# Both heads of a pair in one 128x128 chain matmul, two buffers each for R and K, and new durations in the planner

## The chip, the cores and the metric

The kernel runs on one core of a Trainium2 chip. Five engines of that core work at the same time, each on its own queue: TensorE (PE, matrix multiplications), VectorE (DVE), ScalarE (ACT), GpSimd (POOL) and SyncE (SP), which here issues nearly all the DMA transfers. The time is device microseconds (us) of one execution, and a kernel's time is the median over several executions.

## The reference

One layer of a hybrid encoder trunk takes a step for 512 prompt tokens of a new stream and for 8 running streams of 16 tokens each, 640 tokens in all, model width 1024. All is float32.

```python
h    = rmsnorm(x, norm_g)
proj = h @ w_in                      # columns: q,k,v,z_A | gates g_A,g_B | r,k,v,w-lora,a-lora,z_B
# A: stick-breaking attention, 16 heads of 64
z = q @ k.T / 8
weight[t,s] = sigmoid(z[t,s]) * prod(1 - sigmoid(z[t,j]) for s < j < t)      # s < t only
o_a = weight @ v                     # sample streams also see 128 cached keys
# B: RWKV-7, 16 heads of 64, after a token shift of its columns; w, kk, a from small projections
for t: S = S * w_t - (S kk_t)(kk_t * a_t) + v_t k_t ;  o_t = S r_t
o_b = groupnorm(o_b) + bonus
y   = x + (sig(g_A) * ((o_a silu(z_A)) @ w_o_a) + sig(g_B) * ((o_b silu(z_B)) @ w_o_b)) @ w_out
# out: rmsnorm(y), keys and values, shift rows, the states S
```

## The kernel before

**The projections.** The large products are cut into 97 jobs of 128 output columns. A job loads its weights (`raw`, 128x1024), splits them into a rounded part `whi` (ScalarE) and the rest `wlo` (VectorE, `wlow`), and runs over two halves of the tokens; each half is 8 k-steps of three matmuls, `xh` by `whi`, `xl` by `whi` and `xh` by `wlo`, 128x320, into a PSUM bank `ps_g`. In the trace these are the rows `ps_g<-xh,whi`, `ps_g<-xl,whi` and `ps_g<-xh,wlo`, called projection matmuls below. The weights of the job after this one are split while this one runs: `wlow` is emitted at k-step 5 of the first half.

**The recurrence.** RWKV-7 is computed in chunks of 64 tokens, for a pair `p` of heads at a time (eight pairs; head 0 on partitions 0 to 63, head 1 on 64 to 127). For each pair four generators, here called streams, run:

- `prep`: from the projected `R`, `K`, `V` and the decays to `H` (the decayed keys and queries), `BK` (both kinds of keys, written beside each other), then the intra-chunk products `BK` x `H` on PE, which VectorE masks into `AB` and into the other half of `H`; last the transposes `X` and `BKt`. Between the products stand the norm (`nrm`, `bones`) and the latent matmuls (`wh`, `wl`).
- `prep2`: the inverse of a triangular matrix per chunk. ScalarE copies diagonal blocks of `AB` into `STG`, VectorE turns them (`INV`), GpSimd solves them in small steps, VectorE turns them back into `STG`, PE combines the blocks ("the solve").
- `samp`: the states of the sample streams.
- `chain`: the serial part, one `step` per chunk (the first step takes chunks 0, 8 and 9 together, so 8 steps and 10 chunks). Each step visits PE three times: `X` by `H` into `ps_b` and `ps_c`; after ScalarE has copied the result to `RH`, `RH` by `AB` into `ps_b`; after ScalarE has copied that into `X`, `X` by `BKt` into `ps_b` and `X` by `AB` into `ps_c`. VectorE then forms the next chunk's state in `X` (with `SW`, the decayed old state), and the next step starts. Each product is done per head, as two 64-column matmuls; `ps_c` gathers the outputs, which ScalarE moves to `Oa` after four steps.

`post` then normalises `Oa`. When all pairs are done, the attention follows in the same manner (`aprep`, `attn`): scores `ks` by `qh` and `ql` into `ps_a`, sigmoids `kp` and `bt` on ScalarE, a running product and `bt` times `kp` on VectorE, transposes of `bt` into `ps_b` (a multiplication by the identity in `cst`), and the product with the values. Then come the output projections.

**What sets the order.** The queues hold a fixed program. It is written by a planner: `Clock` (lines 89 to 155) keeps a modelled time for each engine and tile, `_Eng.call` (from line 211) charges a duration for each emitted instruction, and `Driver.run` (from line 283) takes, at PE's modelled time, the stream of the lowest number whose tiles are ready by the model; if none is, it emits the next two k-steps of a projection job. The durations in `Clock` thus place instructions in the queues, and do nothing else. `near` in it is the delay that it takes between two instructions that depend on each other on one engine; `take` gives the next PSUM bank (3 of `ps_g`, 2 each of `ps_a` and `ps_b`, 1 of `ps_c`). A stream can also wait for a flag: `prep` begins when the pair before has set `rkfree`, since `R` and `K` have one buffer each, and the projection jobs of the next pair's `R`, `K` and `V` come up once `rksoon` is set:

```python
        if p > 2:
            yield flag("chain", p - 3)                     # before H is written (three buffers)
...
            g1, s1k = ([], []) if p == 0 else ([("rkfree", p - 1)], [("rksoon", p - 1)])
...
                    if (half, k) == ((0, 5) if i else (1, 1)):
                        wlow(i + 1)
```

Of the kernel before, what the change touches and what calls it, by code (L numbers as in the profile page):

```python
# [33 lines left out]
T = 640  # L34
# [54 lines left out]
class Clock:  # L89
# [114 lines left out]
class _Eng:  # L204
# [3 lines left out]
    def __getattr__(self, op):  # L208
        f = getattr(self.obj, op)

        def call(*a, **k):
# [7 lines left out]
            if e == "pe":  # L219
                w = k.get("lhsT")  # L220
                if w is None:
                    d = 0.115
                else:
                    m = _cols(w)
                    if w.dtype == F32R:
                        d = max(n / 2360.0, 0.107)
                    elif w.dtype == F32:
                        d = max(0.026 + n * 0.00087, 0.082 if m > 32 else 0.041) if m <= 64 else 0.005 + n / 600.0
                    else:
                        d = 0.06  # L230
            elif e == "act":
                d = 0.05 + n * 0.00086 + 0.1 * sum(hasattr(k.get(x), "tensor") for x in ("scale", "bias"))
# [6 lines left out]
            elif e == "dve":  # L239
                d = 0.066 + n * 0.00105  # L240
                if "scalar" in op:
                    d += 0.03 * sum(hasattr(x, "tensor") and _cols(x) == 1 for x in list(a) + list(k.values()))
                if op == "reciprocal":
                    d = 0.05 + n * 0.0064
            elif e == "pool":
                d = 0.15 + n * (0.0021 if op == "tensor_tensor" else 0.001)
                if op == "tensor_copy":
                    d = 0.2 + n * 0.0035
# [72 lines left out]
def body(tc, ins, outs, dbg=None):  # L321
# [157 lines left out]
    def gemm_range(i0, i1):  # L479
# [6 lines left out]
        for i in range(i0, i1):  # L486
# [9 lines left out]
            for half in range(2):  # L496
# [5 lines left out]
                for k in range(8):  # L502
# [12 lines left out]
                    if (half, k) == ((0, 5) if i else (1, 1)):  # L515
                        wlow(i + 1)
# [29 lines left out]
    def start():  # L546
        x34 = pers.tile([128, 2, D], F32, tag="H", name="x34", bufs=3)
        srow = pers.tile([88, 3, 128], F32, tag="AB", name="srow", bufs=3)
# [159 lines left out]
    def prep(p):  # L708
# [9 lines left out]
        if p + 1 < NPAIR:  # L718
            rw[p + 1] = {}
# [16 lines left out]
        yield [K]  # L736
        nrm = tr.tile([128, T], F32, tag="nrm", name="nrm")
# [28 lines left out]
        setf("rksoon", p)  # L766
# [10 lines left out]
        if p > 2:  # L777
            yield flag("chain", p - 3)
            yield flag("schain", p - 3)
        H = o["H"] = pers.tile([128, 2, 10, 128], F32, tag="H", name="H", bufs=3)  # L780
        AB = o["AB"] = pers.tile([128, 10, 128], F32, tag="AB", name="AB", bufs=3)
        BK = tr.tile([128, 10, 2, 64], F32, tag="BK", name="BK")
        c8 = dict(c=8)
        for h in range(2):
            rs = RS[h]
            stt(H[rs, h, 0:8, 0:64], kkn[rs, 0:512].rearrange("p (c t) -> p c t", **c8), -1.0,
                e1p[rs, :, 0:64], ALU.mult, ALU.mult)
            stt(H[rs, h, 8:10, 0:64].rearrange("p g (b t) -> p g b t", b=4),
                kkn[rs, 512:640].rearrange("p (g b t) -> p g b t", g=2, b=4), -1.0,
                e1s[rs, :, 0:16].rearrange("p (g b) t -> p g b t", g=2), ALU.mult, ALU.mult)  # L790
# [15 lines left out]
        for c0, c1 in ((0, 4), (4, 8), (8, 10)):  # L806
# [3 lines left out]
            for c in range(c0, c1):  # L810
                for h in range(2):
                    rs = RS[h]
                    mm(pvs[h][:, c - c0, :], lhsT=BK[rs, c].rearrange("p s t -> p (s t)"),
                       rhs=H[rs, h, c, :], start=True, stop=True)
            for h in range(2):
                rs, op = RS[h], RS[1 - h]
                vtt(AB[rs, c0:c1, :], pvs[h][rs, 0:n],
                    msk[rs].unsqueeze(1).broadcast_to([64, n, 128]), ALU.mult)
                vtt(H[op, h, c0:c1, :], pvs[h][op, 0:n],
                    msk[op].unsqueeze(1).broadcast_to([64, n, 128]), ALU.mult)  # L820
            yield [H]
# [37 lines left out]
    def prep2(p):  # L859
# [17 lines left out]
        tmp = inv.tile([128, 128], F32, tag="itmp", name="itmp")  # L877
# [11 lines left out]
        for q in range(4):  # L889
# [11 lines left out]
        for c in range(8):  # L901
            for q in range(4):
                up = slice(32 * q, 32 * q + 16)
                i = 32 * (q % 2)
                mm(pv[32 * q:32 * q + 32, c], lhsT=AB[up, c, i:i + 32], rhs=Q[up, 0:16, c],
                   start=True, stop=True)
        Y1 = inv.tile([128, 8, 16], F32, tag="itmp", name="Y1")
# [24 lines left out]
        yield [AB, Q]  # L932
# [4 lines left out]
        for c in range(8):  # L937
            for h in range(2):
                a = slice(64 * h, 64 * h + 32)
                b = slice(64 * h + 32, 64 * h + 64)  # L940
                mm(psy[b, c * 32:(c + 1) * 32], lhsT=AB[a, c, 32:64], rhs=Q[a, :, c],
# [7 lines left out]
        for c in range(8):  # L949
            for h in range(2):  # L950
                a = slice(64 * h, 64 * h + 32)
                b = slice(64 * h + 32, 64 * h + 64)
                mm(pst[a, c * 32:(c + 1) * 32], lhsT=Y[b, c, :], rhs=AB[b, c, 32:64],
                   start=True, stop=True)
        for h in range(2):
            a = slice(64 * h, 64 * h + 32)
            V.tensor_copy(AB[a, 0:8, 32:64], pst[a, 0:256].rearrange("p (c s) -> p c s", c=8))
        setf("prep", p)

    def samp(p):  # L960
# [17 lines left out]
        for b in range(8):  # L978
            for h in range(2):
                rs = RS[h]  # L980
                hv = H[rs, h, 8 + b // 4, :].rearrange("p (e b t) -> p e b t", e=2, b=4)
                mm(pv[rs, b], lhsT=S0T[rs, b, :], rhs=hv[:, :, b % 4, :], start=True, stop=True)
        for h in range(2):
            rs = RS[h]
            for g in range(2):
                act(out=H[rs, h, 8 + g, :].rearrange("p (e b t) -> p e b t", e=2, b=4),
# [6 lines left out]
    def chain(p):  # L993
# [11 lines left out]

        def step(js, pos):

# [3 lines left out]
            rh = ps[:, 0:192].rearrange("p (c v) -> p c v", c=3)  # L1011
            u = ps[:, 192:384].rearrange("p (c v) -> p c v", c=3)
# [10 lines left out]
            for c, po in zip(js, pos):  # L1023
                for h in range(2):
                    mm(po[RS[h]], lhsT=H[:, h, c, 64:128], rhs=X[:, c, h, :], start=c == j, stop=False,
                       skip_group_check=True)
            yield [RH, AB]
            for k, c in enumerate(js):
                for h in range(2):
                    rs = RS[h]  # L1030
                    mm(u[rs, k], lhsT=AB[rs, c, 0:64], rhs=RH[rs, k], start=True, stop=True)
            for h in range(2):
                act(out=X[RS[h], j, h, :], in_=u[RS[h], 0], func=AF.Copy)
            if n > 1:
                for h in range(2):
                    V.tensor_copy(X[RS[h], js[1]:js[1] + n - 1, h, :], u[RS[h], 1:n])
            yield [X]
            for h in range(2):
                mm(ps[RS[h], 384:448], lhsT=BKt[:, j, h * 64:(h + 1) * 64], rhs=X[:, j, h, :],
                   start=True, stop=True)  # L1040
            for c, po in zip(js, pos):
                for h in range(2):
                    rs = RS[h]
                    mm(po[rs], lhsT=AB[rs, c, 64:128], rhs=X[rs, c, h, :], start=False, stop=True,
                       skip_group_check=True)
# [711 lines left out]
```

## Time and profile before

| | |
|---|---|
| runs of the kernel | median 1248.35 us (1247.88 to 1251.11, three) |
| the profiled execution | 1252.26 us; span from its first to its last instruction 1250.4 us |
| mean granted clock of TensorE | 0.968 |
| busy: PE | 1157.7 us (93% of the span), 10818 matmul records |
| busy: weight loads / VectorE / ScalarE / GpSimd | 1033.7 / 770.0 (62%) / 626.3 (50%) / 405.9 us (32%) |
| moved by DMA | 130.79 MB |
| start, 0 to 42 us | PE busy 34.1 us |
| recurrent stage with projections, 42 to 840 us | PE busy 754.3 us |
| attention with projections, 840 to 1086 us | PE busy 213.2 us |
| output projections, 1086 to 1250.4 us | PE busy 156.2 us |

All rows are of one profiled execution. A row of the timeline has the start and the duration in us, the engine, line 212 (the helper through which nearly every instruction is issued), the operation, written tile `<-` read tiles, for PE the part of the array in use (128*128, 64*64), the size, and `x` how many like instructions are in the row; in square brackets stands how long the engine had been idle ahead of it and for what. A row of the waits names the waiting engine and tile, then what it waited for: us in total, times, longest.

### The profile page before, as it was taken

How to read it: one execution, taken by the hardware profiler on the slowest of the kernel's cores; microseconds unless marked ns; L12 is line 12 of the kernel's file. 1: busy time of each engine (PE TensorE's matmuls, PEld its weight loads, DVE VectorE, ACT ScalarE, POOL GpSimd, SP SyncE). 2: the span in 40 equal slices, each digit the busy share in tenths (PEclk: the TensorE clock that was granted, in tenths of full speed). 3: DMA queues.
4: the chain of work that ended last, by engine and by line, in shares of the span. 5: the costliest groups of instructions: out<-in, count | busy, mean ns of one | idle time of the engine just before them, and what ended most of it. 6: DMA issues, size and time to landing. Idle time of an engine off the chain costs nothing.

```text
span 1250.4 us, 26994 instructions
## 1 busy us (share of the span) xinstructions
PE 1157.7 (93%) x10818; PEld 1033.7 (83%) x10818; DVE 770.0 (62%) x1501; ACT 626.3 (50%) x1328; POOL 405.9 (32%) x603
## 2 busy tenths in 40 slices
PE   7999899999899999999999999998898887999997
PEld 5989778888788798787787788997777776899997
DVE  5575855776856756756756742337777778654334
ACT  5637267466366474474474463534555453413223
POOL 1034341332432350351352241124444446312302
PEclk9999899999999998898999889999999997999999
DMA  5232131322212232311322322395765565246322
GB/s 193 67 107 62 54 104 47 84 88 83 72 58 77 73 85 65 88 55 58 90 58 70 84 79 80 105 255 155 204 177 143 140 177 158 88 131 185 102 100 84
DMA packets 205300, 130.79 MB, mean 105 GB/s; under 512 B 78332, under 2 KB 184696, under 8 KB 205176
## 3 DMA queue, kind: packets, MB, share of 16 engines
q1 hardware_dynamic: 204888, 129.03, 35.5%
q8 instruction: 85, 1.39, 0.5%
q14 instruction: 39, 0.32, 0.1%
q0 software_dynamic: 288, 0.05, 0.0%
HBM read 97.70 MB, written 31.35 MB: 103 GB/s over the span
## 4 chain that ended last, share of the span: by engine, by line
PE 60%; DVE 18%; ACT 11%; issue 5%; POOL 3%; DMA 2%; SPq 0%; DVEq 0%; ACTq 0%; POOLq 0%
PE ps_g L212 42%; PE ps_a L212 9%; PE ps_b L212 6%; DVE kp L212 4%; PE ps_c L212 3%; ACT STG L212 2%; DVE bt L212 2%; ACT AB L212 2%; DVE BK L212 2%; DVE H L212 1%; DVE wlo L212 1%; ACT L212 1%; DVE STG L212 1%; DVE Oa L212 1%; ACT X L212 1%
## 5 line engine op out<-in xcount | busy, mean ns | idle before, releaser
L212 PE MATMUL ps_g<-xh,whi 128*128 128x320 f32 (+1 forms) x1424 | 481.6, 338 | 0.2 <-ACT xh L212 0.2
L212 PE MATMUL ps_g<-xl,whi 128*128 128x320 f32 (+1 forms) x1424 | 448.0, 315 | 5.5 <-DVE xl L212 5.5
L212 PE MATMUL ps_g<-xh,wlo 128*128 128x320 f32 (+1 forms) x1424 | 447.5, 314 | 1.9 <-DVE wlo L212 1.9
L212 PEld LDWEIGHTS ps_g<-xh,whi 128*128 128x128 f32 x1424 | 274.1, 193 | 20.5 <-issue 5.9
L212 PEld LDWEIGHTS ps_g<-xl,whi 128*128 128x128 f32 x1424 | 274.7, 193 | 9.3 <-DVE xl L212 6.5
L212 PEld LDWEIGHTS ps_g<-xh,wlo 128*128 128x128 f32 x1424 | 274.2, 193 | 2.4 <-DVE wlo L212 2.4
L212 DVE TENSOR_TENSOR wlo<-raw,whi 128x1024 fp32r<-128x1024 f32 x97 | 123.5, 1273 | 37.5 <-ACT whi L212 36.5
L212 ACT ACTIVATE whi<-raw 128x1024 fp32r<-128x1024 f32 x97 | 102.6, 1057 | 69.7 <-PE ps_g L212 39.4
L212 POOL TENSOR_TENSOR itmp<-INV 128x28 f32<-128x28 f32 (+6 forms) x112 | 44.7, 399 | 186.5 <-DVE INV L212 178.4
L212 DVE TENSOR_TENSOR_SCAN kp<-kp,amsk 128x256 f32<-128x256 f32 (+3 forms) x80 | 77.2, 973 | 42.3 <-ACT kp L212 42.2
L212 POOL TENSOR_TENSOR bt<-bt,amsk 128x128 f32<-128x128 f32 x64 | 46.9, 738 | 140.8 <-ACT bt L212 75.6
L212 ACT ACTIVATE RH<-ps_b 128x64 f32<-128x64 f32 (+1 forms) x64 | 15.1, 236 | 119.2 <-PE ps_b L212 119.1
L212 ACT ACTIVATE kp<-ps_a 128x512 f32<-128x512 f32 (+3 forms) x72 | 33.0, 459 | 72.7 <-PE ps_a L212 47.1
L212 ACT ACTIVATE sp<-ps_g 128x320 f32<-128x320 f32 x80 | 35.0, 438 | 68.0 <-PE ps_g L212 50.9
L212 ACT ACT_TABLE_LOAD x44 | 56.5, 1283 | 20.7 <-DVE BK L212 13.5
L212 PE MATMUL ps_b<-cst,bt 128*128 128x128 f32 x192 | 34.9, 288 | 24.9 <-DVE bt L212 22.9
L212 POOL TENSOR_TENSOR ux<-X,cst 128x256 f32<-128x256 f32 x32 | 24.3, 781 | 80.2 <-PE ps_b L212 45.0
L212 DVE SCALAR_TENSOR_TENSOR X<-ps_b,wc,SW 64x64 f32<-64x64 f32 x96 | 27.0, 282 | 37.5 <-PE ps_b L212 35.8
L212 PEld LDWEIGHTS ps_b<-cst,bt 128*128 128x128 f32 x192 | 22.3, 144 | 33.1 <-issue 9.7
L212 DVE TENSOR_TENSOR bt<-bt,kp 128x511 f32<-128x511 f32 (+4 forms) x72 | 43.2, 599 | 8.8 <-POOL bt L212 2.0
L212 POOL TENSOR_TENSOR INV<-INV,itmp 128x28 f32<-128x28 f32 (+6 forms) x112 | 44.8, 400 | 8.8
L212 PE MATMUL ps_g<-olo,mgh 128*128 128x256 f32 x160 | 45.0, 281 | 0.0
(250 smaller groups left out, 2299.9 us busy)
## 6 DMA issues: line engine op xcount, KB each, us to landing
raw<-in_w_in_dram SPq DMA_DIRECT2D x81, 512.0 KB
q<-dr_q SPq DMA_DIRECT2D x32, 160.0 KB
Kr<-in_cache_sb_k_dram SPq DMA_DIRECT2D x16, 256.0 KB
Vp<-in_cache_sb_v_dram SPq DMA_DIRECT2D x16, 256.0 KB
raw<-in_w_o_b_dram SPq DMA_DIRECT2D x8, 512.0 KB
raw<-in_w_o_a_dram SPq DMA_DIRECT2D x8, 512.0 KB
oraw<-in_w_out_dram SPq DMA_DIRECT2D x4, 1024.0 KB
dr_zB<-zm SPq DMA_DIRECT2D x8, 320.0 KB
```

The source lines that it names most:

```text
L212: r = f(*a, **k)
```

## The change

1. **The chain in 128x128 matmuls.** `H` becomes `[128, chunk, part, head, 64]` and `AB` `[128, chunk, part, 128]`, where each head's block stands on the diagonal and the rest is zero. One matmul now takes both heads: all 128 columns of `H` by both heads' `X`. Of the 128x128 result the two blocks on the diagonal are read (`heads`), the other two are not. `RH` is 128 columns wide per chunk. `ps_c` holds four chunks in place of six, so `Oa` is written after 2, 4 and 2 steps, head by head.
2. **`AB` in two fixed tiles** (`ABD`), which GpSimd sets to zero once at the start; before, three buffers in turn. `H` has two buffers for three, and the wait for chain p-2 now stands ahead of writing `H` (it was chain p-3 there, and p-2 behind the products).
3. **Two buffers for `R` and `K`**: the job of `R` waits for `rkfree` of pair p-2 (it was p-1); `rksoon` is set as soon as `K` is there, where it was set after the norm's reciprocals. That brings up the next pair's jobs earlier. `prep` itself begins as before.
4. **`Clock`**: new durations for most operations, a surcharge of 0.1 or 0.2 where a matmul uses another part of the array than the one before it (`mode`), and smaller `near` values.
5. `wlow` is emitted at k-step 3 for 5.

```diff
-        self.near = dict(pe=0.25, act=0.2, dve=0.2, pool=0.15, dma=0.0)
+        self.near = dict(pe=0.25, act=0.15, dve=0.14, pool=0.15, dma=0.0)
...
-                    d = 0.115
+                    d = 0.109
...
+                elif w.dtype == F32:
+                    d = max(0.026 + n * 0.00087, 0.082 if m > 32 else 0.041) if m <= 64 else \
+                        max(n / 600.0 + 0.005, 0.216)
...
+                if mode != self.clk.mode:
+                    d += 0.1 if self.clk.mode == "full" else 0.2
...
-                d = 0.066 + n * 0.00105
...
+                d = 0.075 + n * 0.00106
+                if op == "scalar_tensor_tensor":
+                    d = 0.13 + n * 0.00112
...
+                elif op == "transpose" and len(ins[0].shape) > 2 and ins[0].ap[-1][0] > 1:
+                    d = 2.03
+                if out.shape[0] < 128 and any(_name(x).startswith("ps_") for x in ins if hasattr(x, "tensor")):
+                    d += 0.09
...
-                    if (half, k) == ((0, 5) if i else (1, 1)):
+                    if (half, k) == ((0, 3) if i else (1, 1)):
                         wlow(i + 1)
...
         yield [K]
+        setf("rksoon", p)
...
-        setf("rksoon", p)
...
-        if p > 2:
-            yield flag("chain", p - 3)
-            yield flag("schain", p - 3)
-        H = o["H"] = pers.tile([128, 2, 10, 128], F32, tag="H", name="H", bufs=3)
-        AB = o["AB"] = pers.tile([128, 10, 128], F32, tag="AB", name="AB", bufs=3)
+        if p > 1:
+            yield flag("chain", p - 2)
+            yield flag("schain", p - 2)
+        H = o["H"] = pers.tile([128, 10, 2, 2, 64], F32, tag="H", name="H")
+        AB = o["AB"] = ABD[p % 2]
...
             for k, c in enumerate(js):
-                for h in range(2):
-                    mm(rh[RS[h], k], lhsT=H[:, h, c, 0:64], rhs=X[:, c, h, :], start=True, stop=True)
-            RH = ch.tile([128, 3, 64], F32, tag="RH", name="RH")
-            act(out=RH[:, 0:n], in_=rh[:, 0:n], func=AF.Copy)
+                mm(pv[:, k], lhsT=H[:, c, 0].rearrange("p h t -> p (h t)"), rhs=xs[c], start=True, stop=True)
+            RH = ch.tile([128, 3, 128], F32, tag="RH", name="RH")
+            act(out=RH[:, 0:n], in_=pv[:, 0:n], func=AF.Copy)
...
             for k, c in enumerate(js):
-                for h in range(2):
-                    rs = RS[h]
-                    mm(u[rs, k], lhsT=AB[rs, c, 0:64], rhs=RH[rs, k], start=True, stop=True)
+                mm(u[k], lhsT=AB[:, c, 0], rhs=RH[:, k], start=True, stop=True)
...
-        for steps in (((0, 8, 9), (1,), (2,), (3,)), ((4,), (5,), (6,), (7,))):
+        for steps in (((0, 8, 9), (1,)), ((2,), (3,), (4,), (5,)), ((6,), (7,))):
...
-                    rw[p][n] = pl.tile([128, T], F32, tag=n, name=n, bufs=3 if n == "V" else None)
+                    rw[p][n] = pl.tile([128, T], F32, tag=n, name=n, bufs=3 if n == "V" else 2)
...
-            g1, s1k = ([], []) if p == 0 else ([("rkfree", p - 1)], [("rksoon", p - 1)])
+            g1 = [("rkfree", p - 2)] if p > 1 else []
+            s1k = [("rksoon", p - 1)] if p else []
...
+        ABD = [pers1.tile([128, 10, 2, 128], F32, name=f"AB{i}") for i in range(2)]
...
         G.memset(STG, 0.0)
+        for t in ABD:
+            G.memset(t, 0.0)
```

The durations decide where instructions land, so the queues themselves are shown at three places. First PE, one step of the chain in the middle of the recurrent stage; before:

```order
L212 MATMUL ps_b<-X,H 64x64 x2
L212 MATMUL ps_c<-X,H 64x64 x2
L212 MATMUL ps_g<-xh,whi 128x320
...
L212 MATMUL ps_b<-RH,AB 64x64 x2
L212 MATMUL ps_g<-xh,whi 128x320
...
L212 MATMUL ps_b<-X,BKt 64x64 x2
L212 MATMUL ps_c<-X,AB 64x64 x2
```
and now (`AB_102` is one of the two fixed tiles):

```order
L213 MATMUL ps_b<-X,H 128x128
L213 MATMUL ps_c<-X,H 128x128
L213 MATMUL ps_g<-xh,whi 128x320
...
L213 MATMUL ps_b<-RH,AB_102 128x128
L213 MATMUL ps_g<-xh,whi 128x320
...
L213 MATMUL ps_a<-cst,s0r 128x128 x4
L213 MATMUL ps_g<-xh,whi 128x320
...
L213 MATMUL ps_b<-X,BKt 128x128
L213 MATMUL ps_c<-X,AB_102 128x128
```
Each pair of 64-column matmuls is one of 128 columns; six projection matmuls still stand between the first visit and the second, and six more, a batch of transposes and again six between the second and the third.

Second PE in the attention of the last pair, from the scores of one query block to the next transposes of `bt`; before:

```order
L212 MATMUL ps_a<-ks,qh 128x384
L212 MATMUL ps_a<-ks,ql 128x384
L212 MATMUL ps_b<-cst,bt 128x128 x4
L212 MATMUL ps_a<-ks,qh 128x256
L212 MATMUL ps_a<-ks,ql 128x256
L212 MATMUL ps_b<-cst,bt 128x128 x3
L212 MATMUL ps_g<-xh,whi 128x320
L212 MATMUL ps_g<-xl,whi 128x320
L212 MATMUL ps_g<-xh,wlo 128x320
```
and now:

```order
L213 MATMUL ps_a<-ks,qh 128x384
L213 MATMUL ps_a<-ks,ql 128x384
L213 MATMUL ps_b<-cst,bt 128x128 x4
L213 MATMUL ps_a<-ks,qh 128x256
L213 MATMUL ps_a<-ks,ql 128x256
L213 MATMUL ps_g<-xh,whi 128x320
L213 MATMUL ps_g<-xl,whi 128x320
L213 MATMUL ps_g<-xh,wlo 128x320
...
L213 MATMUL ps_g<-xh,wlo 128x320
L213 MATMUL ps_b<-cst,bt 128x128 x3
```
The three transposes of `bt` stood right behind the scores; now twelve projection matmuls stand between (four of them shown as rows, the cut ones are alike).

Third VectorE, where the `H` and `BK` of pair 5 are made (`E_5731` and `E_5189` are its decays) beside the chain of pair 4, whose `X` rows are the state between two steps; before:

```order
L212 SCALAR_TENSOR_TENSOR H<-kkn,E_5731 64x8x64
L212 SCALAR_TENSOR_TENSOR H<-kkn,E_5731 64x2x64
L212 TENSOR_TENSOR BK<-av,sg 64x10x64
L212 TENSOR_TENSOR BK<-K,sg 64x10x64
L212 SCALAR_TENSOR_TENSOR X<-ps_b,wc,SW 64x64 x2
L212 SCALAR_TENSOR_TENSOR H<-kkn,E_5731 64x8x64
L212 SCALAR_TENSOR_TENSOR H<-kkn,E_5731 64x2x64
L212 TENSOR_TENSOR BK<-av,sg 64x10x64
L212 TENSOR_TENSOR BK<-K,sg 64x10x64
L212 SCALAR_TENSOR_TENSOR kkn<-R,prm,K 128x640
L212 TENSOR_TENSOR wlo<-raw,whi 128x1024
L212 SCALAR_TENSOR_TENSOR X<-ps_b,wc,SW 64x64 x2
```
and now:

```order
L213 SCALAR_TENSOR_TENSOR H<-kkn,E_5189 64x8x64
L213 SCALAR_TENSOR_TENSOR H<-kkn,E_5189 64x2x64
L213 TENSOR_TENSOR BK<-av,sg 64x10x64
L213 TENSOR_TENSOR BK<-K,sg 64x10x64
L213 COPY AB_102<-ps_a 32x8x32 x2
L213 SCALAR_TENSOR_TENSOR kkn<-R,prm,K 128x640
L213 COPY X<-ps_b 64x2x64 x2
L213 TENSOR_TENSOR AB_103<-ps_a,cst 64x8x64
L213 TENSOR_TENSOR H<-ps_a,cst 64x8x64
L213 TENSOR_TENSOR AB_103<-ps_a,cst 64x8x64
L213 TENSOR_TENSOR H<-ps_a,cst 64x8x64
L213 TENSOR_SCALAR X<-ps_b,wc 64x64 x2
```
The two heads' blocks of `H` and `BK` stood apart, ahead of an `X` each; now both stand together ahead of the chain's first step, whose `X` rows come behind the masks (`AB_103` and `H` from `ps_a`) of pair 5's products.

More of the change, by code (lines that the diff above doesn't have):

```diff
@@ L546, in start @@
     def start():
-        x34 = pers.tile([128, 2, D], F32, tag="H", name="x34", bufs=3)
-        srow = pers.tile([88, 3, 128], F32, tag="AB", name="srow", bufs=3)
+        x34 = pers.tile([128, 2, D], F32, tag="H", name="x34")
+        srow = pers.tile([88, 3, 128], F32, tag="V", name="srow", bufs=3)
         with pool("start", bufs=1) as sp:
@@ L863, in prep2 @@
         o = rw[p]
-        AB = o["AB"]
+        AB = [o["AB"][:, :, 0, 64 * (q // 2):64 * (q // 2) + 64] for q in range(4)]
+        ABt = o["AB"]
         for q in range(4):
@@ L868, in prep2 @@
             i = q % 2
-            act(out=STG[rq, :, 0:10], in_=AB[rq, :, 32 * i:32 * i + 32].rearrange("p u t -> p t u"), func=AF.Copy)
+            act(out=STG[rq, :, 0:10], in_=AB[q][rq, :, 32 * i:32 * i + 32].rearrange("p u t -> p t u"), func=AF.Copy)
         yield [STG]
@@ L876, in prep2 @@
         DG = INVB.rearrange("p (b x) -> p b x", b=2)[:, :, 0:512].rearrange("p b (t s) -> p b t s", t=16)
-        tmp = inv.tile([128, 128], F32, tag="itmp", name="itmp")
+        tmp = inv.tile([128, 128], F32, tag="Y", name="itmp")
         for j in range(1, 15):
@@ L904, in prep2 @@
                 i = 32 * (q % 2)
-                mm(pv[32 * q:32 * q + 32, c], lhsT=AB[up, c, i:i + 32], rhs=Q[up, 0:16, c],
+                mm(pv[32 * q:32 * q + 32, c], lhsT=AB[q][up, c, i:i + 32], rhs=Q[up, 0:16, c],
                    start=True, stop=True)
-        Y1 = inv.tile([128, 8, 16], F32, tag="itmp", name="Y1")
+        Y1 = inv.tile([128, 8, 16], F32, tag="Y", name="Y1")
         V.tensor_scalar_mul(out=Y1, in0=pv, scalar1=half[:, 1:2])
@@ L1004, in chain, with heads @@
         S8 = ch.tile([128, 64], F32, tag="S8", name="S8", bufs=2)
+        def heads(t, r):
+            h = RS.index(r)
+            return t[r, ..., h * 64:(h + 1) * 64]
         def step(js, pos):
@@ L1049, in step @@
                 if j == 0:
-                    V.tensor_scalar_mul(out=dst, in0=ps[rs, 384:448], scalar1=wc[rs, 0:1])
+                    V.tensor_scalar_mul(out=dst, in0=heads(pv[:, 2], rs), scalar1=wc[rs, 0:1])
                 else:
-                    stt(dst, ps[rs, 384:448], wc[rs, j:j + 1], SW[rs], ALU.mult, ALU.add)
+                    stt(dst, heads(pv[:, 2], rs), wc[rs, j:j + 1], SW[rs], ALU.mult, ALU.add)
             give(ps)
             yield [X]
-        for steps in (((0, 8, 9), (1,), (2,), (3,)), ((4,), (5,), (6,), (7,))):
+        for steps in (((0, 8, 9), (1,)), ((2,), (3,), (4,), (5,)), ((6,), (7,))):
             pob = yield from take("c")
-            pov = pob[:, 0:384].rearrange("p (c v) -> p c v", c=6)
+            pov = pob.rearrange("p (c v) -> p c v", c=4)
             at0 = steps[0][0]
             for js in steps:
-                yield from step(js, [pov[:, c - at0 if c < 8 else c - 4] for c in js])
+                yield from step(js, [pov[:, c - at0 if c < 8 else c - 6] for c in js])
                 if len(js) > 1:
                     drv.spawn(sstate(p), 1)
-            act(out=Oa[:, at0:at0 + 4, :], in_=pov[:, 0:4], func=AF.Copy)
-            done = list(range(at0, at0 + 4))
+            m = len(steps)
+            for h in range(2):
+                act(out=Oa[RS[h], at0:at0 + m, :], in_=heads(pov[:, 0:m], RS[h]), func=AF.Copy)
+            done = list(range(at0, at0 + m))
             if at0 == 0:
-                act(out=Oa[:, 8:10, :], in_=pov[:, 4:6], func=AF.Copy)
+                for h in range(2):
+                    V.tensor_copy(Oa[RS[h], 8:10, :], heads(pov[:, 2:4], RS[h]))
                 done += [8, 9]
@@ L1598, in program @@
         def program():
-            rw[0] = {}
+            rw.update({p: {} for p in range(NPAIR)})
             rwkv_load(0)
```

104 lines of the change are left out of this document (52 added, 52 removed).

## The prediction

> **What bounds the kernel now.** I read the stretches by engine first, then who waits for whom, then single places in the timeline. In the first fence the rows are stretches of the span (us, then each engine's busy time, the granted clock, the DMA share): the recurrent stage, 42 to 840 us, and the attention stage.
>
> ```profile
> 42.00:840.00 798.00, 754.26 (x7595) 668.84 (x7594) 493.83 (x1070) 434.10 (x916) 248.85 (x412) 0.96 0.28 82
> 840.00:1086.00 246.00, 213.15 (x1882) 182.69 (x1881) 179.27 (x234) 123.35 (x291) 111.41 (x129) 0.97 0.58 155
> PE ps_b L212 <- DVE X L212: 12.3, 7, 2.6
> PE ps_a L212 <- DVE STG L212: 11.5, 7, 2.6
> ...
> PE ps_b L212 <- DVE bt L212: 22.9, 28, 2.0
> ```
>
> PE is busy for 754 of 798 us and for 213 of 246 us; no other engine passes 73%. The order on PE is fixed when the program is built, and behind the last attention row there is only projection work without a gap. So the time is PE's own work, plus PE's waits (798 - 754 = 43.7 us and 246 - 213 = 32.9 us), plus what the clock takes (4% of 798 = 32 us and 3% of 246 = 7 us). The last three rows (waiting tile, awaited, us in total, times, longest) name the waits: for the state `X` that VectorE writes between two chain steps, for the turned matrix `STG` ahead of the solve, and, in the attention stage, for the weights `bt`. What the change is worth is read on PE alone, as work removed and as waits covered.
>
> The clock term belongs to the waits. PE waits 1.84 us for a transpose of 1.95 us; within the next microsecond the granted clock is halved for 6.8 us. (The two rows ahead of it, ten projection matmuls apart, give such a matmul's slot: 1.46 / 10 = 0.146 us.)
>
> ```profile
> 737.75 0.31 PE L212 MATMUL ps_g<-xh,whi 128*128 128x320 f32 x1
> ...
> 739.21 0.31 PE L212 MATMUL ps_g<-xl,whi 128*128 128x320 f32 x1
> 739.41 1.95 DVE L212 STREAM_TRANSPOSE STG<-INV 128x1024 f32<-128x1024 f32 x1 [3.97 <-ACT AB L212]
> 741.51 0.73 PE L212 MATMUL ps_a<-STG,AB 16*32 16x16 f32 x64 [1.84 <-DVE STG L212]
> 739.40:742.70 3.30, 1.46 (x69) 1.19 (x69) 2.30 (x2) 1.82 (x3) 0.19 (x1) 1.00 0.51 199
> 742.70:749.50 6.80, 6.80 (x117) 6.43 (x116) 2.47 (x5) 0.54 (x2) 0.00 (x0) 0.50 0.01 2
> ```
>
> **The chain's matmuls.** One step of `chain` costs PE three visits between projection matmuls. A visit's price is the time from the start of the last projection matmul ahead of it to the start of the second one behind it, less two slots of 0.146 us; the second, because the first one behind a visit is itself late (186.30 - 186.04 = 0.26).
>
> ```profile
> 185.27 0.31 PE L212 MATMUL ps_g<-xh,wlo 128*128 128x322 f32 x1
> 185.51 0.34 PE L212 MATMUL ps_b<-X,BKt 128*64 128x64 f32 x4
> 185.78 0.33 PE L212 MATMUL ps_c<-X,AB 64*64 64x64 f32 x4
> 186.04 0.42 PE L212 MATMUL ps_g<-xh,whi 128*128 128x322 f32 x1
> 186.30 0.30 PE L212 MATMUL ps_g<-xl,whi 128*128 128x322 f32 x1
> ...
> 186.88 0.30 PE L212 MATMUL ps_g<-xh,wlo 128*128 128x322 f32 x1
> 187.12 0.34 PE L212 MATMUL ps_b<-X,H 128*64 128x64 f32 x4
> 187.28 0.29 PE L212 MATMUL ps_c<-X,H 128*64 128x64 f32 x4
> 187.50 0.41 PE L212 MATMUL ps_g<-xh,whi 128*128 128x322 f32 x1
> 187.75 0.31 PE L212 MATMUL ps_g<-xl,whi 128*128 128x322 f32 x1
> ...
> 188.34 0.31 PE L212 MATMUL ps_g<-xh,wlo 128*128 128x322 f32 x1
> 188.58 0.33 PE L212 MATMUL ps_b<-RH,AB 64*64 64x64 f32 x4
> 188.84 0.41 PE L212 MATMUL ps_g<-xh,whi 128*128 128x322 f32 x1
> 189.09 0.31 PE L212 MATMUL ps_g<-xl,whi 128*128 128x322 f32 x1
> ```
>
> That gives 186.30 - 185.27 - 0.29 = 0.74, then 187.75 - 186.88 - 0.29 = 0.58, then 189.09 - 188.34 - 0.29 = 0.46: 1.78 us a step. The 0.58 visit holds two pairs of head matmuls, the 0.46 visit one, and both change the array's mode twice (the numbers behind the engine, 128*64 or 64*64 against 128*128). So a pair of heads takes 0.12 us and a change of mode 0.17 us. The 0.74 visit has two pairs and three changes: 0.24 + 0.51, which agrees. Each matmul is written x2 in the program and stands x4 in the trace, so a float32 matmul is two passes.
>
> Afterwards one matmul serves both heads, 128x128, with no change of mode. No float32 matmul of this kind without a mode change beside it is in the trace. The nearest rows are five 128x128 passes (transposes) among projection matmuls, (961.05 - 960.21 - 0.29) / 5 = 0.109 us a pass, so 0.218 us a matmul; and one real float32 matmul of 128x128, two passes, that lies behind a change of mode and takes 932.90 - 932.58 = 0.32:
>
> ```profile
> 960.21 0.31 PE L212 MATMUL ps_g<-xh,wlo 128*128 128x320 f32 x1
> 960.35 0.71 PE L212 MATMUL ps_b<-cst,vT 128*128 128x128 f32 x5
> 960.81 0.40 PE L212 MATMUL ps_g<-xh,whi 128*128 128x320 f32 x1
> 961.05 0.31 PE L212 MATMUL ps_g<-xl,whi 128*128 128x320 f32 x1
> ...
> 932.58 0.49 PE L212 MATMUL ps_a<-kT,qbd 128*128 128x128 f32 x2
> 932.90 0.22 PE L212 MATMUL ps_a<-bfc 128*128 128x128 bf16 x1
> ```
>
> Per head pair `chain` issues 48 two-head matmuls (seven steps of 5 and one of 13). Before: 7 x 1.78 plus the triple step, 1.78 + 8 x 0.12 = 2.74, is 15.2 us, times 8 is 122 us. After: 48 x 0.218 x 8 = 84 us, so -38. Counted the other way, the built program has 283 changes of mode on PE where it had 675, since some visits shared theirs with other narrow matmuls: 392 x 0.17 = 67 us less, and 384 x (0.218 - 0.12) = 38 us more, so -29. I take -30; the ends are -38 and, at 0.32 a matmul, 384 x 0.32 - 122 = +1.
>
> [...]
>
> **The waits in the recurrent stage.** With `R` and `K` doubled and the new durations in `Clock`, producers are issued further ahead of their consumers. Counted in the built program between the second transpose into `STG` and the solve's first matmul: 8 to 14 projection matmuls before, 19 to 33 now; from `BK` to the intra-chunk products: mostly 6 to 18, now 12 to 60; from the evacuation of `RH` and `X` to the next chain visit 6 mostly, now 6 or 12. Twelve more at 0.146 us are 1.8 us, about the 1.84 us waited above. I take the 11.5 us for `STG` down to 1. The waits for `X` come from VectorE's queue:
>
> ```profile
> 597.38 3.27 DVE L212 SCALAR_TENSOR_TENSOR H<-kkn,E 64x512 f32<-64x512 f32 x2
> 600.57 1.05 DVE L212 TENSOR_TENSOR BK<-av,sg 64x640 f32<-64x640 f32 x1
> 601.54 1.79 DVE L212 TENSOR_TENSOR BK<-K,sg 64x640 f32<-64x640 f32 x1
> 603.26 0.59 DVE L212 SCALAR_TENSOR_TENSOR X<-ps_b,wc,SW 64x64 f32<-64x64 f32 x2
> 603.67 0.50 PE L212 MATMUL ps_b<-X,H 128*64 128x64 f32 x3 [2.19 <-DVE X L212]
> L212 DVE TENSOR_TENSOR H<-ps_a,cst 64x512 f32<-64x512 f32 x32 | 22.0, 689 | 0.4
> ```
>
> One head's `H` and `BK` of the next pair, 3.27 + 1.05 + 1.79 = 6.1 us, stand ahead of `X`. Before, this block lies inside the running chain for all seven pairs that have a chain beside them; now for one clearly (pair 6), in the others between two chains, though the masks of the products (the last row, 0.69 us each) then stand in the chain's first step. 12.3 us becomes 4. Of the other 20 us I keep half, and add 6 for new waits: the next pair's norm and latent matmuls now take PSUM banks between two batches of products and wait for VectorE's masks. 43.7 becomes 21, so -23. Ends: -38 and +10.
>
> **The clock.** With the waits halved, 32 us becomes 18: -14; in attention -3. Ends: -35 and +5. [...] The row above, half clock right behind a wait of 1.84, decides for me.
>
> **The attention stage.** Between its first and last score rows stand 691 projection matmuls instead of 613, 78 x 0.146 = 11.4 us of PE work, most of it inside the burst in which PE waits for `bt`; the number of transposes that follow a VectorE product with nothing between falls from 19 to 8. I take -9 of the 22.9 us. Ends: -20 and 0.
>
> **What costs nothing.** The two zeroings of `AB` stand on GpSimd's queue at the start, ahead of its first row below, for which that engine has waited 27.6 us. `RH` is evacuated 64 times at twice the width, and `Oa` in 48 pieces on ScalarE and 16 on VectorE where 24 stood; at about 0.24 us a piece (the `RH` row) this is some 10 and 4 us, on engines that are 54% and 62% busy in this stage, and five table loads go. SyncE issues as many DMAs as before; the cached keys stand nearer to their use (at least 1.8 us of PE work, was 2.8), a load for which PE does not wait in this trace. The wait for chain p-2 ahead of `H` (it was p-3) is met before `H` is written, since that chain ends before pair p's products are due; if it were not, products, solve and chain p would queue up behind it.
>
> ```profile
> 36.06 1.01 POOL L212 TENSOR_TENSOR wl<-wd,wh 128x256 fp32r<-128x256 f32 x1 [27.61 <-ACT wh L212]
> L212 ACT ACTIVATE RH<-ps_b 128x64 f32<-128x64 f32 (+1 forms) x64 | 15.1, 236 | 119.2 <-PE ps_b L212 119.1
> ```
>
> **Sum.** -30 - 23 - 14 - 3 - 9 = -79 on a profiled execution of 1252.26 us (span 1250.4); that run is 3.9 above the median of 1248.35, from which I count: 1169.
>
> **Rivals.** (a) The waits only move: a chain step stands later, VectorE is late for something else, and only the array work goes. Against it are the larger distances; for it that one `H` of 64x512 takes 3.27 / 2 = 1.6 us there and 0.7 in the new `Clock`. 1248 - 30 = 1218, or with a third of the waits 1200. (b) The two-pass price is 0.32: 1248 + 1 - 49 = 1200. [...] (d) Slower: in the first step of each chain `X` queues behind a head's `H` and `BK` and four masks of the next pair. It decides from 79 / 7 = 11.3 us a pair. As measured above it is 6.1 + 4 x 0.69 and a half clock of 6.8 us, which costs 3.4: 12.3 us, so 7 x 12.3 - 79 = +7, 1255. For it: pair 6 has that order. Against: the other six have not. (e) Nearly all waits and clock losses go: -38 - 38 - 35 - 20 = -131, so 1117.
>
> **Chances.** Forecast, 1142 to 1195: 0.60. (a) 0.16, (b) 0.06, (c) 0.03, (d) 0.06, (e) 0.09. The range, 1140 to 1214, takes in (a) and (b) and leaves out (c), (d) and most of (e). A measurement here tells 0.3% (3.7 us) from no change: faster 0.91, same 0.03, slower 0.06.
>
> **What would show it.** Right: `X,H` rows 128*128 with about 0.22 us to the next start; PE's waits for `STG` near 0 and for `X` under 6 us; a granted clock of 0.98 in the recurrent stage; the attention stage with less than 25 us of PE idle. Wrong: a chain pass well over 0.11 us; new rows in which PE waits for `H`, `nrm` or a PSUM bank with more than 20 us together; a clock that stays at 0.96 although the waits went.

## The result, and the profile after

The changed kernel takes 1172.39 us (median of four runs, 1171.08 to 1175.92); the kernel before, run beside it, 1249.73 us. The ratio is 0.9386, with a 95% interval of 0.9359 to 0.9412: 77 us less, where 79 were forecast. The profiled execution took 1171.08 us, span 1169.3, at a mean granted clock of 0.990 (it was 0.968).

The first fence has the two stretches of the changed kernel that answer to those of before, the recurrent stage up to the first score and the attention. The second has PE's longest waits in the recurrent stage (waiting tile, awaited, us, times, longest), then that for `X`, and last the one for `bt` in the attention.

```profile
42.00:796.00 754.00, 728.59 (x6921) 689.45 (x6919) 480.76 (x1089) 442.47 (x942) 236.56 (x412) 0.99 0.30 88
796.00:1028.60 232.60, 217.48 (x1958) 190.36 (x1958) 176.90 (x243) 123.87 (x289) 105.02 (x129) 0.99 0.62 170
```

```profile
PE ps_b L213 <- POOL sn L213: 8.9, 5, 3.9
PE ps_a L213 <- DVE STG L213: 4.4, 2, 3.0
PE ps_a L213 <- POOL wl L213: 3.3, 3, 2.7
...
PE ps_b L213 <- DVE X L213: 1.0, 3, 0.5
...
PE ps_b L213 <- DVE bt L213: 11.8, 18, 1.9
```

PE idles 754.0 - 728.6 = 25.4 us in the recurrent stage (it was 43.7) and 15.1 us in the attention (32.9). The waits for `X`, `STG` and `bt` fell from 12.3, 11.5 and 22.9 us to 1.0, 4.4 and 11.8; a new one came up, 8.9 us for `sn`, the states of the sample streams. The chain looks as forecast, without a change of mode, here two of its visits:

```profile
206.86 0.30 PE L213 MATMUL ps_g<-xh,wlo 128*128 128x322 f32 x1
207.00 0.38 PE L213 MATMUL ps_b<-X,H 128*128 128x128 f32 x2
207.22 0.39 PE L213 MATMUL ps_c<-X,H 128*128 128x128 f32 x2
207.37 0.39 PE L213 MATMUL ps_g<-xh,whi 128*128 128x322 f32 x1
207.60 0.31 PE L213 MATMUL ps_g<-xl,whi 128*128 128x322 f32 x1
...
208.19 0.31 PE L213 MATMUL ps_g<-xh,wlo 128*128 128x322 f32 x1
208.34 0.38 PE L213 MATMUL ps_b<-RH,AB 128*128 128x128 f32 x2
208.48 0.39 PE L213 MATMUL ps_g<-xh,whi 128*128 128x322 f32 x1
208.71 0.31 PE L213 MATMUL ps_g<-xl,whi 128*128 128x322 f32 x1
```

By the prediction's own reckoning the visits take 207.60 - 206.86 - 0.29 = 0.45 and 0.23 us, where they took 0.58 and 0.46; a matmul is 0.22 us, as assumed.

### The profile page after: what moved, and what is told of

It reads as the page before. It is cut to its first block, busy times and chain, and to the rows that moved or that the text cites. A ratio compares the mean times of both kernels' runs of the same rounds, so it can differ in the third digit from the quotient of the medians.

```text
span 1169.3 us, 25426 instructions
## 1 busy us (share of the span) xinstructions
PE 1111.5 (95%) x10050; PEld 1037.7 (89%) x10050; DVE 746.2 (64%) x1517; ACT 629.8 (54%) x1347; POOL 390.5 (33%) x605
## 5 line engine op out<-in xcount | busy, mean ns | idle before, releaser
L213 PE MATMUL ps_g<-xh,whi 128*128 128x320 f32 (+1 forms) x1424 | 468.5, 329 | 1.7 <-ACT xh L213 1.3
L213 PE MATMUL ps_g<-xl,whi 128*128 128x320 f32 (+1 forms) x1424 | 443.5, 311 | 3.3 <-DVE xl L213 3.3
L213 PE MATMUL ps_g<-xh,wlo 128*128 128x320 f32 (+1 forms) x1424 | 443.0, 311 | 1.4 <-DVE wlo L213 1.4
L213 PEld LDWEIGHTS ps_g<-xl,whi 128*128 128x128 f32 x1424 | 270.9, 190 | 6.4 <-DVE xl L213 4.5
L213 PEld LDWEIGHTS ps_g<-xh,wlo 128*128 128x128 f32 x1424 | 270.0, 190 | 2.4 <-DVE wlo L213 2.4
L213 DVE TENSOR_TENSOR_SCAN kp<-kp,amsk 128x256 f32<-128x256 f32 (+3 forms) x80 | 73.6, 929 | 27.8 <-ACT kp L213 27.7
L213 POOL TENSOR_TENSOR bt<-bt,amsk 128x128 f32<-128x128 f32 x64 | 44.0, 691 | 124.3 <-ACT bt L213 81.5
L213 ACT ACTIVATE RH<-ps_b 128x128 f32<-128x128 f32 (+1 forms) x64 | 19.4, 302 | 77.8 <-PE ps_b L213 77.4
L213 POOL TENSOR_TENSOR on<-on,V 128x640 f32<-128x640 f32 x8 | 12.4, 1550 | 108.9 <-ACT on L213 108.9
L213 PE MATMUL ps_b<-cst,bt 128*128 128x128 f32 x192 | 33.5, 278 | 12.4 <-DVE bt L213 11.8
L213 PE MATMUL ps_g<-ohi,mgh 128*128 128x256 f32 x160 | 45.0, 281 | 0.0
```

The lines of the kernel that those rows point to most:

```text
L213: r = f(*a, **k)
```

## The experiments

Times are medians; the ratio is to the kernel before, run in the same series.

| kernel | durations | R, K | chain | us | ratio (95%) |
|---|---|---|---|---|---|
| before | old | one | per head | 1249.7 | 1 |
| changed | new | two | 128x128 | 1172.4 | 0.9386 (0.9359 to 0.9412) |
| e1 | old | two | 128x128 | 1258.1 | 1.0073 (1.0049 to 1.0098) |
| e2 | new | one | per head | 1213.2 | 0.9713 (0.9690 to 0.9736) |
| e3 | new | two | per head, same order | 1184.1 | 0.9481 (0.9458 to 0.9504) |
| e4 | new | one | 128x128 | 1244.2 | 0.9957 (0.9939 to 0.9975) |

**e3, the array term by itself.** Each chain matmul is issued as two, charged to the planner as one, so every queue keeps its order:

```diff
-                mm(u[k], lhsT=AB[:, c, 0], rhs=RH[:, k], start=True, stop=True)
+                for h in range(2):      # in short; charged once, as the 128x128 matmul
+                    nc.tensor.matmul(u[k][RS[h], h * 64:(h + 1) * 64],
+                                     lhsT=AB[RS[h], c, 0, h * 64:(h + 1) * 64], rhs=RH[RS[h], k, 0:64], ...)
```

> The changed kernel with each 128x128 chain matmul issued as two matmuls of one head (64 columns each) at the same place; every queue keeps its order, only RH is again copied 64 columns wide. This isolates the array term. Theory of the prediction: 392 changes of mode cost more than half the array time saves, so it is slower by 20 to 35 us, 1192 to 1207. Rival (array time alone counts): faster by up to 38 us, 1134. Rival (PE hides both): 1172 within 4 us.

1184.11 us, 11.7 above the changed kernel. The sign is the prediction's, the size is not: 12 us, not 20 to 35. The built program of e3 has 646 changes of mode, the changed one 283. With 384 matmuls at 0.22 for pairs at 0.12 us (38 us), 11.7 us make 363 changes cost 50 us, 0.14 each by this estimate, where visits that stand alone gave 0.17.

**e1, the old durations in the changed kernel**, with the old `near` values and without `mode`:

```diff
-        self.near = dict(pe=0.25, act=0.15, dve=0.14, pool=0.15, dma=0.0)
+        self.near = dict(pe=0.25, act=0.2, dve=0.2, pool=0.15, dma=0.0)
...  (and the durations of before)
```

> The changed kernel with the old durations, the old distances between dependent instructions and no surcharge for a change of mode in the planner; all else (128x128 chain, two buffers for R and K, wlo earlier) stays. Theory: the covers of PE's waits come from the durations, so with them gone most of the 35 us of waits and of the 28 us of half clock come back: 1172 + 45 = 1215 us, waits for STG over 8 us, clock 0.97. Rival: the covers come from the second buffers of R and K and the shorter chain; then 1172 to 1182 us and the clock stays at 0.98 or more.

1258.05 us: the new durations carry the whole gain here, and more than the theory gave them. Stretch and waits of its recurrent stage:

```profile
42.00:782.00 740.00, 673.26 (x6401) 625.56 (x6400) 471.80 (x1077) 422.80 (x909) 234.00 (x412) 0.96 0.26 78
```

```profile
PE ps_b L212 <- POOL sn L212: 17.2, 6, 8.0
PE ps_b L212 <- DVE X L212: 12.9, 8, 8.1
PE ps_b L212 <- ACT RH L212: 8.2, 7, 2.1
...
PE ps_a L212 <- DVE STG L212: 3.3, 5, 1.2
```

PE idles 66.7 us in it. The place is not the one expected: `STG` has only 3.3 us; the waits stand in the chain itself (`X`, `RH`) and at the states of the sample streams (`sn`).

**e2, the new durations alone**, in the kernel before.

> The kernel before with the new durations in the planner alone; chain per head, one buffer each for R and K. Theory: the durations are worth about half of the waits and the clock also without the other parts, 1248 - 30 = 1218 us. Rival: without room for the next pair's R and K there is nothing to put into the gaps, so the waits only move: 1240 to 1255 us.

1213.22 us, 37 less, where the theory said 30: the rival falls. Not all of it comes the way the theory had it: PE's idle time over the whole span fell from 92.7 to 68.5 us, by a quarter and not by half, and the clock rose only from 0.968 to 0.972.

**e4, one buffer for R and K again:**

```diff
-            g1 = [("rkfree", p - 2)] if p > 1 else []
-            s1k = [("rksoon", p - 1)] if p else []
+            g1, s1k = ([], []) if p == 0 else ([("rkfree", p - 1)], [("rksoon", p - 1)])
...  (one buffer, and rksoon behind the reciprocals)
```

> The changed kernel with one buffer each for R and K and their gates as before (next pair's R waits for this pair's products to be issued, the jobs come up after the reciprocals). Theory: the second buffers only help the durations to find projection work, so a fifth of the 79 us comes back: 1172 + 15 = 1187 us. Rival: they carry the waits, 1172 + 45 = 1217 us. Rival: they carry nothing, 1172 within 4 us.

1244.24 us: 72 of the 77 us are gone. The theory is out by a factor of five; the second option, 45 us, is nearest and still short, and PE's waits in the recurrence are only a part of it. The fence counts projection matmuls (x) from the first chain product of pair 0 to that of pair 7, in before, e2, e4, the changed kernel and e1:

```profile
142.20:755.40 613.20, 406.94 (x2293) 0.96 0.25 74
143.70:751.10 607.40, 406.18 (x2347) 0.95 0.26 76
152.60:762.40 609.80, 428.09 (x2516) 0.97 0.27 80
150.10:703.40 553.30, 379.26 (x2258) 0.99 0.28 81
159.00:688.10 529.10, 302.87 (x1734) 0.95 0.23 67
```

With one buffer each for `R` and `K` the seven pairs take 607 to 613 us, whatever the durations, the chain and the buffers of `H`, and while PE gets through 2293 to 2516 projection matmuls beside them. So the recurrence has a pace of its own, some 87 us a pair, that PE's work doesn't set; with two buffers it is 76 to 79 (81 in e3). A cheaper chain at the old pace only lets PE use up its projection work sooner. In e4 it then lacks in the attention. The row of 21.6 us is the end of the attention, between the last projection matmul and the first output projection:

```profile
862.00:1104.00 242.00, 211.30 (x1858) 181.88 (x1856) 179.26 (x246) 119.41 (x274) 105.77 (x130) 0.95 0.53 143
1083.20:1104.80 21.60, 17.39 (x150) 12.77 (x148) 15.67 (x24) 12.82 (x31) 7.53 (x11) 0.83 0.18 47
1104.70:1242.50 137.80, 119.56 (x864) 116.65 (x864) 58.49 (x125) 35.53 (x73) 38.13 (x44) 0.91 0.39 132
```

```profile
PE ps_g L213 <- POOL oAh L213: 6.1, 2, 5.2
```

There PE runs narrow work alone at a clock of 0.83, and the output projections behind it run at 0.91 and wait for their operand `oAh`. This lack is not the whole loss. Against the changed kernel PE idles 46 us more: 20 in the recurrent stage (42 to 862 us, 820 - 774.7 = 45.3 us idle, where it was 25.4), 16 in the attention and 11 in the output projections; and the clock of 0.958 takes 52 us of the span in place of 12. The gate, the flag and the buffers were moved together; which of the three holds the pace is not separated.

**e5, PE's waits for STG filled** in the kernel before, to test what halves the clock:

```diff
         ps = yield from take("a")
         pv = ps[:, 0:128].rearrange("p (c s) -> p c s", c=8)
+        for _ in range(3):
+            nc.tensor.matmul(ps[:, 128:448], lhsT=ident, rhs=cst[:, 0:320], start=True, stop=True)
```

> The kernel before with three spare float32 matmuls (128x320, of constants, into an unused part of the bank) on PE's queue ahead of each solve; nothing else moves. PE's waits for STG (11.5 us in 7 places, four of them followed by half clock, 31 us of it in all) are filled with work that takes about as long (24 matmuls, at about 0.5 us each 13 us). Theory (idle time within a short stretch halves the clock): those half-clock episodes go, worth about 13 us, against some 3 us of longer occupation: 1249 - 10 = 1239 us and the clock up by 0.01. Rival (the half clock is not due to these waits): 1249 to 1253 us, clock 0.968.

1246.04 us, ratio 0.9961 (0.9944 to 0.9979), clock 0.975: 4.8 us less, though 24 spare matmuls were added. Here is the solve of pair 7, which the prediction showed with its 1.84 us of waiting and 6.8 us of half clock (PE rows, then stretches, then the wait):

```profile
735.03 1.78 PE L902 MATMUL ps_a<-cst 128*128 128x320 f32 x6
737.00 0.74 PE L212 MATMUL ps_a<-STG,AB 16*32 16x16 f32 x64 [0.19 <-DVE STG L212]
735.00:738.40 3.40, 3.21 (x77) 2.35 (x76) 2.30 (x2) 1.77 (x3) 0.12 (x1) 1.00 0.51 198
738.40:745.20 6.80, 5.98 (x153) 5.37 (x153) 2.92 (x7) 0.97 (x3) 0.00 (x0) 1.00 0.01 2
PE ps_a L212 <- DVE STG L212: 2.9, 6, 1.0
```

The clock stays at 1.00, and so at two more of the solves that had been followed by half clock (from 124 to 134 and from 561 to 575 us); all four were waits of the same kind, now filled. The gain is half of the 10 us expected: the clock takes (1 - 0.975) x 1245.7 = 31.1 us of this execution's span, where it took 40.0, 9 us less and not the 13 expected; where the rest went was not shown.

**e6, wlo at k-step 5 again** (`(0, 3)` to `(0, 5)`).

> The changed kernel with wlo emitted at k-step 5 of the first half again. Theory: VectorE has room for it at either place, so the time stays at 1172 within 4 us. Rival: with the chain closer to VectorE's limit the later wlo meets the masks and PE waits for it: over 10 us of waits for wlo, 1182 us or more.

1175.77 us, 0.9407 (0.9386 to 0.9428): not told apart from the changed kernel, as the theory has it; PE waits 2.7 us for `wlo`.

**Towards a faster version.** The new wait for `sn` has its origin in the planner. An operand that an instruction overwrites in place isn't counted as read, so `gtt(sn, sn, ...)` on GpSimd is planned before VectorE has written `sn`. On the chip VectorE comes to it behind four masks (the last two of them and `sn` on VectorE, then GpSimd and PE):

```profile
243.56 0.69 DVE L213 TENSOR_TENSOR AB<-ps_a,cst 64x512 f32<-64x512 f32 x1
244.26 0.68 DVE L213 TENSOR_TENSOR H<-ps_a,cst 64x512 f32<-64x512 f32 x1
244.87 0.67 DVE L213 TENSOR_TENSOR sn<-ps_b,S0T 128x512 f32<-128x512 f32 x1
245.62 1.04 POOL L213 TENSOR_TENSOR sn<-sn,wc 128x512 f32<-128x512 f32 x1 [3.88 <-DVE sn L213]
246.72 1.11 PE L213 MATMUL ps_b<-cst,sn 128*128 128x128 f32 x4 [3.92 <-POOL sn L213]
```

Five kernels went after this and the other waits; each is the changed kernel with:

```diff
-            ins = [x for x in aps if x is not out]                                        # v1, v2
+            ins = [x for x in aps if x is not out] + [out] * (sum(x is out for x in aps) > 1)
-                g2, s2 = [("post", p - 3)], s2 + [("chain", p - 3)]                       # v2
+                g2, s2 = [("post", p - 3)], s2 + [("post", p - 3)]
-        gtt(sn, sn, wc[:, 8:16]...)                                                       # v5, v6
+        gtt(sn, sn[:, :, :], wc[:, 8:16]...)
-            m = n - 2                                                                     # v4, v6
+            m = n - 3          # and five buffers of bt, the product with the values one later
```

> The changed kernel with one correction in the planner: an operand that is read and written in place by one instruction counts as read. In the changed kernel the planner takes the in-place product sn on GpSimd as ready before VectorE has written sn, and PE waits 8.9 us for it in five places. Theory: these waits and the half clock behind the longest (6.8 us at half speed) go: 1172 - 11 = 1161 us, waits for sn under 2 us. Rival: other instructions move too and the waits come up elsewhere, 1172 within 4 us.

> As the one before, and the projection job of V comes up only when the pair whose V buffer it takes is through post (it came up after that pair's chain and then stood at the head of the jobs, waiting, with no other projection matmul to issue). Theory: the stretches in which PE has narrow work without a projection matmul between (411 to 421 and 571 to 581 us of the changed kernel, 5.6 us of waits) go: 5 us below the one before, 1156 us. Rival: V comes later and holds up its pair: 1165 us or more.

> The changed kernel with the in-place product sn on GpSimd, and only that one, counted by the planner as reading what VectorE wrote. Theory: the 8.9 us of waits for sn go as they did when all in-place operands were corrected, and the first pair is not put off (its first chain step stays near 150 us; with all corrected it stood at 168): 1172 - 9 = 1163 us. Rival: any shift of the order gives as much as it takes: 1168 to 1176 us.

> The changed kernel with the transposes of bt in the attention one score block later (three blocks behind the scores for two, and five buffers of bt for four). Theory: the 10.6 us of waits for bt fall under 3 us, 1172 - 8 = 1164 us. Rival: fewer projection matmuls stand between, as the planner finds the transposes ready at once, and VectorE, busy for 170 of 240 us there, keeps the same pace: 1172 within 4 us.

> The two changes above together. Theory: they lie in different stages and add up, 1172 - 17 = 1155 us. Rival: no more than the better of the two.

None is faster, and none reaches the time of its theory: v1 1175.54 us (0.9409, 0.9389 to 0.9429), v2 1191.48 (0.9538, 0.9517 to 0.9558), v5 1178.65 (0.9418, 0.9401 to 0.9434), v4 1180.54 (0.9433, 0.9416 to 0.9450), v6 1186.82 (0.9491, 0.9467 to 0.9515). In v1 0.6 us of waits for `sn` is left and in v5 none, and as much came up elsewhere, in v5 3.9 us for `AB` and 4.5 for `X`. In v2 the later `V` slows the recurrence, and the attention runs out of projection work as in e4 (the first row below; clock 0.84). In v4 the wait for `bt` became one for the gate's product `sg`:

```profile
1030.00:1052.00 22.00, 17.37 (x151) 12.66 (x150) 15.68 (x24) 12.87 (x31) 7.66 (x11) 0.84 0.18 46
PE ps_c L213 <- DVE sg L213: 10.5, 8, 2.4
PE ps_b L213 <- DVE bt L213: 6.8, 5, 1.4
```

The last run, v7, leaves the order alone and fills the longest waits with spare matmuls, as e5 did:

```diff
+        for _ in range({0: 5, 4: 2}.get(p, 0)):              # second part of the solve
+            nc.tensor.matmul(ps[:, 256:512], lhsT=ident, rhs=cst[:, 0:256], start=True, stop=True)
...
+        for _ in range({1: 6, 2: 1, 4: 2, 6: 2}.get(p, 0)):  # ahead of the transposes of sn
+            nc.tensor.matmul(ps[:, 0:320], lhsT=ident, rhs=cst[:, 0:320], start=True, stop=True)
```

> The changed kernel with spare float32 matmuls of constants on PE's queue in the places where it waits longest in the recurrent stage: five and two of 128x256 ahead of the second part of the solve of pairs 0 and 4 (waits of 2.9 and 1.3 us for STG), and six, one, two and two of 128x320 ahead of the transposes of sn of pairs 1, 2, 4 and 6 (waits of 3.9, 0.9, 1.8 and 1.9 us). Together about 9 us of spare work inside 12.6 us of waits; no queue is otherwise changed. Theory (idle time within a short stretch halves the clock): the half clock behind three of these waits goes (3.4, 6.8 and 3.4 us, worth 6.8): 1172 - 6 = 1166 us at a clock of 0.99 or more. Rival (the half clock has another cause): 1172 to 1175 us.

1168.48 us (1166.49 to 1169.39), ratio 0.9348 (0.9332 to 0.9365). All five runs lie below the four of the changed kernel, though the two intervals overlap a little: some 4 us less, the fastest version here. Of the three half-clock stretches two are gone, those that began at 143.0 and 245.4 us. The third, at pair 4's solve, is still there (last row), although PE idles for only 0.7 us in the stretch ahead of it, where it also runs the solve's 32x32 matmuls; so for that one the theory failed.

```profile
PE ps_b L213 <- POOL sn L213: 2.5, 5, 0.7
PE ps_a L213 <- DVE STG L213: 1.5, 2, 0.8
466.30:469.70 3.40, 2.68 (x42) 2.19 (x41) 2.49 (x12) 2.25 (x5) 0.00 (x0) 1.00 0.67 209
469.70:473.10 3.40, 3.40 (x15) 3.40 (x14) 3.27 (x13) 0.00 (x0) 0.00 (x0) 0.50 0.11 41
```

## Why the prediction was right, and where it was not

The total is right to 3.4 us, the terms less so. Two came out smaller and two larger than forecast, and their errors cancel; that the total is so close is luck.

- **Array time, -30.** Mis-sized. e3 gives -12. PE's time in the trace less idle time and half clock fell by 19 us from before to the changed kernel, between the same two projection matmuls (the 72nd and the 4168th). Counted so, e3 lies 15 us above the changed kernel, since it idles 4 us less and loses 3 us more to the clock; so 12 to 15 us are array time, and 4 to 7 come from the order itself, with fewer changes of mode. The step that was mis-sized is the price of a change of mode, 0.17 us from visits that stand alone; over all of them it is 0.14. That array time alone counts, the first rival in e3, is refuted by its sign.
- **Waits in the recurrent stage, -23.** -18 (43.7 to 25.4). `X` fell further than thought and `STG` less; the new waits were put at 6 us, and `sn` alone is 8.9, in a place that was not named. Rival (d), `X` behind `H`, `BK` and masks, did not come: 1.0 us.
- **Clock, -17.** (1 - 0.968) x 1250.4 = 40.0 us lost before, (1 - 0.990) x 1169.3 = 11.7 after: -28. The link to the waits is shown by e5 (1.00 at the three solves named there) and by two of the three stretches in v7. The size, taken in proportion to the waits, was too small. The half clock in the prediction's rows begins 1.2 us behind the end of the wait (742.70 against 741.51), not within one.
- **Attention, -9.** -18 (32.9 to 15.1), near the end of -20.
- **"What costs nothing".** `wlo` and the zeroings hold. The wait for chain p-2 ahead of `H` was said to be met before: it is not. In these rows of VectorE for pair 2, `K` is ready at 198 us, but `H` and `BK` are written from 214, behind chain 0's last state `S`:

```profile
197.15 0.85 DVE L213 TENSOR_TENSOR K<-K,nrm 128x640 f32<-128x640 f32 x1
211.01 0.57 DVE L213 SCALAR_TENSOR_TENSOR S<-ps_b,wc,SW 64x64 f32<-64x64 f32 x2
214.18 0.88 DVE L213 SCALAR_TENSOR_TENSOR H<-kkn,E 64x512 f32<-64x512 f32 x2
214.99 0.81 DVE L213 TENSOR_TENSOR BK<-av,sg 64x640 f32<-64x640 f32 x1
215.72 0.81 DVE L213 TENSOR_TENSOR BK<-K,sg 64x640 f32<-64x640 f32 x1
PE ps_a L213 <- DVE H L213: 1.7, 4, 0.8
```

  PE lost 1.7 us to `H` in all. Whether a third buffer of `H` would quicken the pairs wasn't tried.
- **What the prediction did not see** is how the parts depend on each other. It credited "`R` and `K` doubled and the new durations" together with longer distances and read everything on PE. Neither carries it alone: durations -37 (e2), everything but the durations +8 (e1), everything but the buffers -5 (e4). The buffers set the pace of the pairs, the durations keep PE fed at that pace.

## What to carry to other kernels

Before a cheaper step is credited with its saving, look at how long the loop around it takes in kernels or stages where the busy engine has less to do: if the period stays (607 to 613 us here), a buffer or a gate sets it. Work that covers other work is a stock: count what is left of it when the last stage that needs it begins. And a short wait on PE costs more than its length when the clock halves behind it (6.8 us at 0.50 behind a wait of 1.84 us, in the kernel before), so a spare matmul in a wait that can't be removed is worth trying, since it moves nothing else; it took the half clock away in five of the six places shown here.

## What the runs showed of the hardware

**When the clock halves.** In the changed kernel's profile it does so, apart from its start and its end, at 143.0, 245.4, 474.1 and 948.6 us, the second time for 6.8 us and the others for 3.4. Here are the 3.4 us ahead of each of these four, with the stretch at half clock behind the first, and last 3.4 us that had no effect, as the clock is 1.00 behind them too, from 661.8 to 665.2 us (PE's busy time is the second figure, the clock the third from the right):

```profile
139.60:143.00 3.40, 1.45 (x33) 1.23 (x34) 2.60 (x10) 2.01 (x4) 0.52 (x1) 1.00 0.02 5
143.00:146.40 3.40, 3.40 (x20) 3.06 (x22) 3.31 (x7) 0.53 (x1) 0.00 (x0) 0.50 0.00 0
242.00:245.40 3.40, 0.80 (x8) 0.23 (x6) 3.12 (x5) 0.00 (x0) 0.00 (x0) 1.00 0.02 5
470.70:474.10 3.40, 1.97 (x38) 1.57 (x36) 2.53 (x10) 2.18 (x5) 0.00 (x0) 1.00 0.39 112
945.20:948.60 3.40, 1.71 (x15) 1.05 (x16) 3.40 (x4) 0.10 (x1) 1.12 (x1) 1.00 0.91 325
658.40:661.80 3.40, 1.50 (x11) 1.50 (x12) 0.95 (x2) 3.29 (x8) 1.04 (x1) 1.00 0.24 96
```

PE is idle for 1.95, 2.60, 1.43 and 1.69 us of the four stretches that were followed by half clock, and for 1.90 us of the one that was not. So idle time alone doesn't give a sharp bound. In the profile of the kernel before, PE is idle for 0.77 to 2.53 us of the 3.4 us ahead of each of the thirteen half-clock stretches between its start and its end; in the row of v7 it is 0.7 us. The first, third and fourth here and that of v7 also hold matmuls on a part of the array (32*32 or 128*32), the one without effect holds none; whether those count as less work, no run tested. One kernel's time goes with its clock from run to run: v6 took 1184.29 us at a clock of 0.979 and 1194.30 at 0.971. Why the clock differs from one execution to the next was not shown.

**VectorE beside GpSimd.** One head's `H` and `BK` took 6.1 us in the prediction's row, while GpSimd was busy for 5.88 of 5.95 us (597.38 to 603.33), the last 4.77 us of its work there being for the same `H`. In the rows of pair 2 above, behind GpSimd's part, they take 0.88 + 0.81 + 0.81 = 2.5 us. GpSimd is done with its `H` by then, and idle for those 2.35 us (214.18 to 216.53):

```profile
207.69 3.22 POOL L213 TENSOR_TENSOR H<-R,E 64x512 f32<-64x512 f32 x4 [9.59 <-PE ps_c L213]
```

In the changed kernel, too, the group took 3.25 + 1.05 + 1.79 = 6.1 us where GpSimd was busy beside it for 6.22 of 6.30 us (pair 1, 133.8 to 140.1 us), so the new layout of `H` is not the reason. That the 3.6 us between the two come from GpSimd's work is the author's estimate from these rows; no run changed this alone.
